# Refilling buffers two tiles further ahead in a LayerNorm and GELU kernel that streams 128 MB

## The chip, the cores and the metric

The kernel runs on one core of one Trainium2 chip. The metric is the device time of one execution in microseconds (us), taken as the median of several executions. The span that the profile gives, from the first to the last instruction, is 1.7 to 1.8 us shorter than the time. "The trace" below is the record of one execution: instructions, DMA packets, and the semaphore updates that tell when a transfer has landed.

## The reference, cut to what matters

```python
mean = np.mean(x, axis=-1, keepdims=True)             # x: 8 x 1024 x 2048 float32
var = np.var(x, axis=-1, keepdims=True)
normalized = (x - mean) / np.sqrt(var + eps)
out = gamma * normalized + beta
return 0.5 * out * (1 + np.tanh(np.sqrt(2 / np.pi) * (out + 0.044715 * out ** 3)))
```

The input is 64 MB and the output is 64 MB. As 128-row tiles of 128 x 2048 float32 these are 64 tiles of 1 MB each way.

## The kernel before

Twenty tile buffers (`NB = 20`) rotate. A tile is loaded into its buffer, its mean and variance are taken there (VectorE, and ScalarE for one tile in four of most groups), VectorE writes (x - mean) * gamma to PSUM, TensorE adds the beta term, ScalarE applies the GELU back into the same buffer, and SyncE stores the buffer. SyncE issues all loads and stores, in program order:

```python
NB = 20
LAG = 4
...
def load(i):
    xt = xin.tile([P, d], F32, name="xt")
    nc.sync.dma_start(out=xt, in_=xf[i * P:(i + 1) * P])          # L53
    xts[i] = xt
...
for i in range(NB):
    load(i)
...
def gelu(j):
    g, k = of_tile[j]
    nc.scalar.activation(out=xts[j], in_=ps[j % 2], func=ACTF.Gelu_apprx_tanh,
                         scale=rstds[g][0][:, k:k + 1])            # L151
    nc.sync.dma_start(out=of[j * P:(j + 1) * P], in_=xts[j])       # L153
    nxt = j + NB - LAG
    if NB <= nxt < ntiles:
        load(nxt)
```

Behind the store of tile j stands the load of tile j+16. It goes into the buffer of tile j-4, so it may start only when the store of tile j-4 has landed. SyncE waits there, and whatever stands behind that load in its list waits with it.

## Time and profile before

| | before |
|---|---|
| time, median of the first 3 runs | 325.29 us (324.59 to 325.31) |
| span of the profiled run | 323.2 us |
| busy: DVE, PE, ACT, POOL | 85%, 80%, 63%, 41% |
| packet time of the DMA queue, share of 16 engines | 98.8% |
| traffic | 134.2 MB, 415 GB/s over the span |
| landing of the last store | 322.24 us |

The first reading is that DMA is full and no compute engine is. The lines of the profile themselves stand in the prediction.

### The profile page before, as it was taken

To read this page: it belongs to the slowest core of one execution; us is meant where nothing else is said; L and a number is where in the kernel's file an instruction comes from. 1 tells how busy PE (TensorE), PEld (TensorE's weight loads), DVE (VectorE), ACT (ScalarE), POOL (GpSimd) and SP (SyncE) were. 2 spreads that over 40 slices of the span, in tenths; PEclk is the share of its full clock that TensorE was granted. 3 is DMA by queue.
4 is the path that set the end of the run, shared out by engine and by line. 5 is a ranking of instruction groups with operands and counts; after the bars stand their busy time and mean duration, and the time that the engine had idled before them with its cause. 6 is when DMAs were issued, how large, how long until landed. Compare 5 with 4: busy or idle time off the path is not lost.

```text
span 323.2 us, 2327 instructions
## 1 busy us (share of the span) xinstructions
PE 258.3 (80%) x528; PEld 100.9 (31%) x528; DVE 276.3 (85%) x315; ACT 203.7 (63%) x188; POOL 132.2 (41%) x319
## 2 busy tenths in 40 slices
PE   5978548888888888988888877858988588888890
PEld 2423223333333333333333323323333133333330
DVE  2989968989999999999999969966998789997520
ACT  1237557678778686868777776744687476544552
POOL 0732231827180807171635342050361505488800
PEclk9999958999999999999999999978999799999998
DMA  7999999999999999999999999999999999999994
GB/s 295 425 424 422 422 419 425 428 410 429 427 428 426 427 427 425 428 425 426 427 427 428 425 429 430 421 427 431 424 429 428 426 425 429 426 426 426 425 394 197
DMA packets 18450, 134.39 MB, mean 416 GB/s; under 512 B 2050, under 2 KB 2050, under 8 KB 2050
## 3 DMA queue, kind: packets, MB, share of 16 engines
q1 hardware_dynamic: 18432, 134.23, 98.8%
q8 instruction: 4, 0.07, 0.1%
q14 instruction: 10, 0.08, 0.1%
q10 hardware_dynamic: 4, 0.02, 0.0%
HBM read 67.13 MB, written 67.11 MB: 415 GB/s over the span
## 4 chain that ended last, share of the span: by engine, by line
DVE 46%; DMA 25%; PE 9%; issue 8%; POOL 5%; ACT 4%; DVEq 0%; SPq 0%; POOLq 0%; ACTq 0%
DVE ps L142 26%; DMA xt<-in_x_dram 24%; DVE st L100 18%; PE ps L146 5%; PE ps L75 4%; ACT xt L151 3%; DVE mv L102 2%; POOL t L127 2%; DMA g_t<-in_gamma_dram 1%; POOL std L130 1%; POOL y L129 1%; ACT b_t L76 1%; POOL t L126 1%; POOL t L128 1%; ACT w L136 0%
## 5 line engine op out<-in xcount | busy, mean ns | idle before, releaser
L146 PE MATMUL ps<-b_t,w 128*128 128x512 f32 x512 | 244.3, 623 | 53.0 <-DVE ps L142 43.0
L151 ACT ACTIVATE xt<-ps,y 128x2048 f32<-128x2048 f32 x64 | 125.9, 1967 | 89.5 <-PE ps L146 87.1
L142 DVE SCALAR_TENSOR_TENSOR ps<-xt,mv,g_t 128x2048 f32<-128x2048 f32 x64 | 149.4, 2334 | 18.1 <-ACT xt L151 16.7
L146 PEld LDWEIGHTS ps<-b_t,w 128*128 128x128 f32 x512 | 95.7, 196 | 202.3 <-issue 120.9
L100 DVE BATCH_NORM_STATS2 st<-xt 128x6 f32<-128x512 f32 x200 | 125.9, 672 | 13.2 <-DMA xt<-in_x_dram 13.0
L112 POOL TENSOR_SCALAR mv<-sq 128x1 f32<-128x1 f32 x14 | 8.7, 619 | 117.2 <-ACT junk L111 117.2
L126 POOL TENSOR_TENSOR t<-y 128x4 f32<-128x4 f32 (+2 forms) x60 | 48.3, 805 | 4.8
L111 ACT ACTIVATE junk<-xt,mv 128x2048 bf16<-128x2048 f32 x14 | 27.9, 1991 | 0.0
L106 ACT ACTIVATE junk<-xt 128x2048 bf16<-128x2048 f32 x14 | 26.6, 1900 | 0.0
L136 ACT ACTIVATE w<-ident,std 128x128 f32<-128x128 f32 x64 | 20.5, 389 | 9.4 <-POOL std L130 9.4
L127 POOL TENSOR_TENSOR t<-t,ve 128x4 f32<-128x4 f32 (+2 forms) x60 | 22.3, 372 | 4.7
L128 POOL TENSOR_SCALAR t<-t 128x4 f32<-128x4 f32 (+2 forms) x60 | 21.8, 364 | 5.2
L122 POOL TENSOR_SCALAR ve<-mv 128x4 f32<-128x4 f32 (+2 forms) x20 | 4.6, 231 | 34.4 <-DVE mv L102 34.0
L129 POOL TENSOR_TENSOR y<-y,t 128x4 f32<-128x4 f32 (+2 forms) x60 | 14.0, 234 | 5.0
L102 DVE BATCH_NORM_AGGREGATE mv<-st 128x2 f32<-128x24 f32 x50 | 13.2, 264 | 2.8
L75 PE MATMUL ps<-g_t,ones 1*128 1x512 f32 x8 | 7.2, 1072 | 3.7 <-DMA g_t<-in_gamma_dram 3.7
L75 PE MATMUL ps<-b_t,ones 1*128 1x512 f32 x8 | 7.0, 1056 | 0.0
L76 ACT ACTIVATE g_t<-ps 128x2048 f32<-128x2048 f32 x1 | 1.9, 1877 | 7.8 <-PE ps L75 7.8
L130 POOL TENSOR_TENSOR std<-ve,y 128x4 f32<-128x4 f32 (+2 forms) x20 | 6.0, 302 | 1.6
L123 POOL TENSOR_SCALAR y<-ve 128x4 int32<-128x4 int32 (+2 forms) x20 | 6.0, 299 | 1.7
L76 ACT ACTIVATE b_t<-ps 128x2048 f32<-128x2048 f32 x1 | 1.9, 1877 | 4.9 <-PE ps L75 4.9
L75 PEld LDWEIGHTS ps<-g_t,ones 1*128 1x128 f32 x8 | 2.5, 325 | 6.8 <-issue 6.8
(11 smaller groups left out, 10.3 us busy)
## 6 DMA issues: line engine op xcount, KB each, us to landing
xt<-in_x_dram SPq DMA_DIRECT2D x64, 1024.0 KB, 19.7
out_dram<-xt SPq DMA_DIRECT2D x64, 1024.0 KB, 19.6
g_t<-in_gamma_dram ACTq DMA_DIRECT2D x1, 8.0 KB
b_t<-in_beta_dram ACTq DMA_DIRECT2D x1, 8.0 KB
```

What stands on the lines that cost most here:

```text
L75: nc.tensor.matmul(pt[:, s], lhsT=ones[0:1, :], rhs=row[0:1, s], start=True, stop=True)
L100: nc.vector.bn_stats(out=sts[i][:, c, :], in_=xts[i][:, c * BANK:(c + 1) * BANK])
L102: nc.vector.bn_aggr(out=slot(i), in_=sts.pop(i))
L106: nc.scalar.activation(out=junk, in_=xts[i], func=ACTF.Identity, scale=-1.0 / d, accum_out=slot(i)[:, 0:1])
L111: nc.scalar.activation(out=junk, in_=xts[i], func=ACTF.Square, bias=slot(i)[:, 0:1], accum_out=sq)
L126: po.tensor_tensor(out=t, in0=y, in1=y, op=MUL)
L127: po.tensor_tensor(out=t, in0=t, in1=ve, op=MUL)
L128: po.tensor_scalar(out=t, in0=t, scalar1=-0.5, scalar2=1.5, op0=MUL, op1=ADD)
L136: nc.scalar.activation(out=w, in_=ident, func=ACTF.Identity, scale=rstds[g][1][:, k:k + 1])
L142: nc.vector.scalar_tensor_tensor(out=pt, in0=xts[j], scalar=mvs[g][:, k, 0:1], in1=g_t, op0=ADD if j in on_scalar else SUB, op1=MUL)
L146: nc.tensor.matmul(pt[:, s], lhsT=wts[j], rhs=b_t[:, s], start=False, stop=True, skip_group_check=True)
L151: nc.scalar.activation(out=xts[j], in_=ps[j % 2], func=ACTF.Gelu_apprx_tanh, scale=rstds[g][0][:, k:k + 1])
```

## The change

The intent is to ask for a tile earlier: behind the store of tile j SyncE loads tile j+18, into the buffer that tile j-2 leaves. Loads then run two tiles further ahead of the stores, and two fewer stores stand ahead of each of these later loads, called refills below.

```diff
     NB = 20
-    LAG = 4
+    LAG = 2
     GAP, SLACK = 3, 7
```

## The prediction

> **What bounds the kernel now.** I read four views in this order: the page, the table of stages by window, the waits of SyncE's queue, and the chain that ended last. The page first: which resource is full.
>
> ```profile
> PE 258.3 (80%) x528; PEld 100.9 (31%) x528; DVE 276.3 (85%) x315; ACT 203.7 (63%) x188; POOL 132.2 (41%) x319
> ...
> DMA  7999999999999999999999999999999999999994
> ...
> q1 hardware_dynamic: 18432, 134.23, 98.8%
> ...
> xt<-in_x_dram SPq DMA_DIRECT2D x64, 1024.0 KB, 19.7
> out_dram<-xt SPq DMA_DIRECT2D x64, 1024.0 KB, 19.6
> ```
>
> The reader is to see that the 16 DMA engines are full from the second slice to the last but one, that one queue carries everything (64 loads and 64 stores of 1 MB), and that VectorE, the busiest compute engine, is 15% idle. Each transfer takes some 19.7 us from issue to landing. The trace records when each one landed: the first load at 6.08 us, the last store at 322.24, so 127 steps in 316.16 us, 2.49 us each. One engine's share of a transfer is 8 packets of 8 KB, and the median packet takes 0.309 us: 8 x 0.309 = 2.47 us. So from first landing to last there is almost no slack. 19.7 / 2.47 = 8.0 transfers are in flight.
>
> Then where the DMA engines are not full (columns: window; its length; busy time and count for PE, PEld, DVE, ACT, POOL; the clock; the DMA share; GB/s):
>
> ```profile
> 100.00:260.00 160.00, 132.46 (x280) 51.81 (x279) 147.90 (x168) 112.06 (x103) 63.35 (x144) 0.97 1.01 427
> 260.00:312.00 52.00, 45.18 (x100) 17.69 (x99) 42.56 (x41) 30.32 (x27) 29.59 (x61) 1.00 1.01 426
> 312.00:318.00 6.00, 3.01 (x8) 0.98 (x6) 0.00 (x0) 2.69 (x2) 0.00 (x0) 1.00 0.67 279
> 318.00:323.20 5.20, 0.00 (x0) 0.00 (x0) 0.00 (x0) 0.00 (x0) 0.00 (x0) 0.71 0.45 186
> ```
>
> Only the last 11 us show idle DMA time: 0.33 x 6.0 + 0.55 x 5.2 = 4.8 us on the mean of the 16 engines. This is all that an earlier load could win back, if anything can.
>
> Then why SyncE issues when it does (waiter <- what ended it: us in total, times, longest):
>
> ```profile
> SPq L53 <- DMA xt<-in_x_dram: 95.4, 48, 2.1
> SPq L153 <- DMA out_dram<-xt: 85.9, 42, 2.7
> SPq L153 <- ACT xt L151: 47.5, 17, 5.5
> ...
> SPq L53 <- DMA out_dram<-xt: 3.6, 2, 2.5
> ```
>
> A load (L53) waits for an earlier load 48 times, and for a store only twice, although the code makes it wait for the store that leaves its buffer. The trace tells which: the load of tile 45, issued at 172.94, follows the landing of the load of tile 41 at 172.87, eight transfers earlier in SyncE's order. Every transfer n waits for transfer n-8 here, as the eight completion semaphores are used in turn. The buffer wait is hidden behind that: load j+16 needs store j-4, nine places earlier, which has landed by then.
>
> Last, the chain, in order of time (start, length, what):
>
> ```profile
> 232.27 19.80 DMA xt<-in_x_dram
> 252.09 0.69 DVE st L100
> 252.79 2.27 DVE ps L142
> ...
> 311.34 3.69 PE ps L146 x8
> 315.05 1.97 ACT xt L151
> ```
>
> From 172.94 to 252.09 the chain is load after load. At 252.09 the load of tile 57 lands, VectorE has waited 2.73 us for it, and from there compute runs to the last Gelu at 317.02, 64.9 us later. The last store is then issued and lands 5.2 us later. The chain says that the end hangs on when tile 57 arrives. I don't follow it there, for the reason under "the end" below.
>
> **What the Trainium skill says.** "DMA: Bandwidth & Descriptors", section "Why a DMA increments its semaphore by 16 and not by 1", says that a transfer's engines finish independently and that only the full count means landed. The trace agrees: the sixteen completions of the store of tile 61 came between 312.55 and 317.33 us, 4.8 us apart. The same page, section "Anatomy of one DMA", says "DMA engines do not wait on semaphores" and that the wait lies in the issuing sequencer; the trace agrees, with 181 us of SyncE waits on earlier transfers while the DMA share stays at 1.01. Its section "Bandwidth" has 425 GB/s for a 16 MB load on a lone core; this trace holds 426 to 427 with loads and stores mixed, so there is no higher rate to hope for. "Perfetto Trace Analysis", section "What 'DMA-bound' means", lists being bound on specific DMA engines as one case. My argument turns on that.
>
> **The change, part by part.** Instructions of the four compute engines stand in the same order in both kernels; only SyncE's list moves: three stores instead of five stand before the first refill, and eighteen instead of sixteen after the last load. No byte and no instruction is added.
>
> *The wait.* With LAG 2 SyncE's order is store j-2, load j+16, store j-1, load j+17, store j, load j+18, and the last waits for the first, five places earlier. This wait now binds in place of the eight-deep one. When it ends, four transfers are left in the queue, then a load and a store go out together: 4 to 6 in flight in place of 8. Landing should take about 4 to 5 transfers, 10 to 12.5 us, in place of 19.7. That alone saves and costs nothing as long as no DMA engine runs dry.
>
> *Does one run dry?* Four transfers are 4 x 2.47 = 9.9 us of work for the engine that is last. The others are ahead by up to 4.8 us (from the spread above), so they have at least 5.1 us left. A new transfer's overhead, read from the last store, which met mostly empty engines, is: issue 317.04 to the middle completion 320.81 = 3.77 us, less 2.47 of data, 1.3 us. 5.1 is well above 1.3. The thinnest place is the first refill: store 0 lands at 56.06 with only stores 1 and 2 behind it, the middle completions of which came at 57.62 and 60.05. Load 20 goes out at 56.13 as before, needed by about 59; store 3 follows 0.4 us later, and load 21 when store 1 lands, at 58.50. Some 1.5 to 2 us to spare there. Cost: 0.
>
> *The loads.* Each refill has two fewer stores ahead of it, so it lands 2 x 2.47 = 4.9 us earlier: tile 57 at 247.1 instead of 252.07. VectorE's wait at tile 45 (2.56 us) should vanish; those at tiles 49 and later shift with the loads. Compute then ends at 317.0 - 4.9 = 312.1.
>
> *The stores.* They go out later, and buffers spend their time as finished output waiting for SyncE instead of in the DMA queue. No compute waits for a store: Gelu writes in place, and only a load needs the buffer back.
>
> *The end.* Here I chose between two readings of those last 11 us. The mean engine is idle for 4.8 us, but the landing of a store is that of its slowest engine: stores 61, 62 and 63 landed at 317.33, 319.83 and 322.24, steps of 2.50 and 2.41 us, which is full pace. The middle completions of the same stores came at 313.70, 316.54 and 320.81, with gaps. So one engine, 4.8 us behind (it took instruction fetches between its packets: one of 8 KB at 283.16 us, where the spread grows from 3.57 to 4.21), works without a pause to the end, and its 128 x 8 packets are the same after the change. Compute ending at 312.1 fills the pauses of the other engines, which then finish near 311.26 + 3 x 2.45 = 318.6 (from the middle completion of store 60), and the slow one still lands the last store at about 322.2. Gain: 0, up to 3.6 us only if the lag itself shrank.
>
> Sum: 0 (bulk) + 0 (queue depth) + 0 to -3.6 (end, most likely near 0) = 325.3, and I take 0.3 off for the chance of the latter: 325.0 us.
>
> **The rivals.** *The end follows compute.* If the last store's pace were set by its issue, the 4.9 us of earlier compute would come through up to the 3.6 us above: about 321.7 us. For it: the chain, and the idle shares of 0.33 and 0.55. Against: the full-pace steps of the last landings. I give it one in eight. *The shallow queue runs dry.* If SyncE's wait cost a pause for each refill of, say, 0.3 us, 43 of them make 13 us: 338 us. For it: SyncE now stands behind a store's completion, and nothing else can be issued meanwhile. Against: the 5.1 us left against 1.3. I give it 3%. *Stores held back stall compute.* Compute would wait if a buffer came free too late, but the refill comes earlier in the order, not later, and tile 45's wait goes. That would give the same 325.
>
> **Range and chances.** The three runs before spread over 0.7 us. The lag of one engine can differ by one instruction fetch, about 0.7 us either way. With one in eight for the first rival, 323.0 to 326.3 should hold it 8 times in 10. Even full success of that rival is -1.1%, so faster by over 2% (below 318.8) has 1%; slower has 3%; within 2% has 96%.
>
> **What would show it.** Right: landing times of 10 to 13 us; loads that now wait mostly for a store; the DMA share at 1.01 up to about 316 us or beyond, and then a sharper fall; the last Gelu some 5 us earlier (312); the last stores' landings still 2.4 to 2.5 us apart; the span near 323. Wrong: DMA shares below 1.0 in the middle (the queue ran dry), or the last landing near 318.6 (the lag was a product of the deep queue, not of the engine).

## The result, and the profile after

| | before | after |
|---|---|---|
| time, median of 6 runs each | 325.26 us (324.59 to 325.43) | 324.14 us (324.06 to 324.63) |
| span of the profiled run | 323.2 us | 322.4 us |
| last GELU ends | 317.02 us | 311.83 us |
| last store lands | 322.24 us | 321.43 us |

The ratio is 0.9975, with a 95% interval of 0.9962 to 0.9988. Ratios are the mean time of one kernel's runs over that of the other's runs of the same rounds, so they are not quite the ratio of the medians in the table. Executions over 1.5% slower than the fastest of the same kernel are left out of the means. By the 2% rule the two kernels are the same; a small difference of about 0.8 us is outside the noise.

The page after, the parts that answer to those shown of before (DMA share by slice, the queue, the transfers with their time from issue to landing):

```profile
DMA  7999999999999999999999999999999999999994
...
q1 hardware_dynamic: 18432, 134.23, 99.0%
...
xt<-in_x_dram SPq DMA_DIRECT2D x64, 1024.0 KB, 12.3
out_dram<-xt SPq DMA_DIRECT2D x64, 1024.0 KB, 14.4
```

The DMA engines are as full as before, and each transfer spends 12 to 14 us on its way in place of 19.7. So the queue is shorter, five or six transfers in place of eight, and nothing was lost by it.

The stages by window (columns as in the prediction):

```profile
100.00:260.00 160.00, 135.81 (x289) 53.10 (x290) 151.79 (x172) 116.81 (x109) 67.26 (x144) 0.98 1.01 427
260.00:312.00 52.00, 44.11 (x96) 17.07 (x96) 38.74 (x38) 28.66 (x23) 29.29 (x61) 1.00 1.01 427
312.00:318.00 6.00, 0.00 (x0) 0.00 (x0) 0.00 (x0) 0.00 (x0) 0.00 (x0) 0.56 0.92 391
318.00:322.40 4.40, 0.00 (x0) 0.00 (x0) 0.00 (x0) 0.00 (x0) 0.00 (x0) 0.50 0.10 43
```

The third window in two parts:

```profile
312.00:316.00 4.00, 0.00 (x0) 0.00 (x0) 0.00 (x0) 0.00 (x0) 0.00 (x0) 0.59 1.01 426
316.00:318.00 2.00, 0.00 (x0) 0.00 (x0) 0.00 (x0) 0.00 (x0) 0.00 (x0) 0.50 0.76 320
```

The middle holds the same 427 GB/s. In the window from 312 to 318 all compute is over, where before PE and ACT still worked, and the DMA share has risen from 0.67 to 0.92; the engines are full up to 316 us. In return it falls to 0.10 in the last window: most DMA engines are done, and the core waits for the last one. The earlier compute bought a fuller tail for the engines that were not the last.

SyncE's waits after (waiter <- what ended it: us in total, times, longest):

```profile
SPq L53 <- DMA out_dram<-xt: 178.3, 44, 14.5
SPq L53 <- DMA xt<-in_x_dram: 25.0, 12, 2.2
...
SPq L153 <- ACT xt L151: 13.0, 10, 3.9
```

Now each of the 44 refills waits for a store, which only 2 did before. SyncE spends 178 us in that wait and it costs nothing, since the DMA engines work meanwhile.

Parts of the chain that ended last, after (start, length, what):

```profile
234.58 12.30 DMA xt<-in_x_dram
246.90 0.69 DVE st L100
...
309.86 1.97 ACT xt L151
```

The load of tile 57 lands at 246.9 us and not at 252.1, and the whole compute tail moves with it, by 5.2 us. The time moved by about 1. This is what the next part tests.

### The profile page after: what moved, and what is told of

The parts are those of the page before. It is cut to its first block, busy times and chain, and to the rows that moved or that the text cites. A ratio compares the mean times of both kernels' runs of the same rounds, so it can differ in the third digit from the quotient of the medians.

```text
span 322.4 us, 2297 instructions
## 1 busy us (share of the span) xinstructions
PE 257.6 (80%) x528; PEld 100.5 (31%) x528; DVE 276.0 (86%) x315; ACT 203.7 (63%) x188; POOL 135.8 (42%) x319
## 4 chain that ended last, share of the span: by engine, by line
DVE 59%; PE 11%; DMA 9%; issue 9%; POOL 5%; ACT 4%; DVEq 0%; POOLq 0%; SPq 0%; ACTq 0%
DVE ps L142 33%; DVE st L100 23%; PE ps L146 6%; DMA out_dram<-xt 4%; PE ps L75 4%; DMA xt<-in_x_dram 4%; ACT xt L151 4%; DVE mv L102 2%; POOL t L127 2%; DMA g_t<-in_gamma_dram 1%; POOL std L130 1%; ACT b_t L76 1%; POOL y L129 1%; POOL t L126 1%; POOL t L128 1%
## 5 line engine op out<-in xcount | busy, mean ns | idle before, releaser
L126 POOL TENSOR_TENSOR t<-y 128x4 f32<-128x4 f32 (+2 forms) x60 | 54.3, 904 | 4.8
L129 POOL TENSOR_TENSOR y<-y,t 128x4 f32<-128x4 f32 (+2 forms) x60 | 16.1, 268 | 5.0
L127 POOL TENSOR_TENSOR t<-t,ve 128x4 f32<-128x4 f32 (+2 forms) x60 | 16.0, 267 | 4.7
L130 POOL TENSOR_TENSOR std<-ve,y 128x4 f32<-128x4 f32 (+2 forms) x20 | 8.1, 407 | 1.6
## 6 DMA issues: line engine op xcount, KB each, us to landing
xt<-in_x_dram SPq DMA_DIRECT2D x64, 1024.0 KB, 12.3
out_dram<-xt SPq DMA_DIRECT2D x64, 1024.0 KB, 14.4
```

What stands on the lines that cost most here:

```text
L126: po.tensor_tensor(out=t, in0=y, in1=y, op=MUL)
L127: po.tensor_tensor(out=t, in0=t, in1=ve, op=MUL)
```

## The experiments

Eleven kernels ran, in three groups; kernels of one group shared a chip and the runs of the kernel before. Landing times are read from the sixteen completions that the trace records for each transfer, one from each DMA engine; "lands" means the last of them, and "the middle" is their median. The trace doesn't number the engines. That the same one comes last from transfer to transfer is read from its even steps and the slowly growing spread of the completions.

**Theory.** The end is set by the DMA engine that finishes last, which works through its 128 shares of 8 packets without a pause. LAG moves waits and compute about, and the time does not follow as long as that engine is fed and compute does not end too late. **Rivals.** Compute's end sets the time. A shorter queue lowers the rate. The small gain comes from something else than the loads.

### Compute's end on the other side: LAG 6 and LAG 5

```diff
-    LAG = 2
+    LAG = 6
```

> LAG 6: the store that a load waits for is thirteen places back and never binds; the queue is eight deep as before; loads land two stores, 4.9 us, later than before. If compute's end counts on this side, it moves from 317.0 to 321.9 us, the last store lands 3.8 to 5.2 us later, at 325.7 to 327.1, and the time is about 328.5 to 330 (+1.2%). If the DMA engines alone set the end: 325.3 again.

Measured: 328.93 us (328.25 to 329.84, 4 runs), ratio to before 1.0125 (1.0107 to 1.0143). Its trace, the end of the chain and the last two windows:

```profile
320.13 1.97 ACT xt L151
```

```profile
312.00:318.00 6.00, 5.25 (x12) 2.30 (x13) 2.36 (x1) 4.14 (x3) 0.42 (x3) 1.00 0.60 249
318.00:326.90 8.90, 2.09 (x5) 0.57 (x3) 0.00 (x0) 1.97 (x1) 0.00 (x0) 0.75 0.57 236
```

The last GELU ends at 322.1 us, and the last store lands at 325.97, 3.85 us after it was issued. All sixteen completions of that store come within 0.15 us, so no DMA engine has a backlog any more: compute ends so late that the late engine has caught up, as far as these times tell. Here compute sets the end.

LAG 5 (the same edit with 5) is the step between.

> LAG 5: loads land one store, 2.5 us, later than before. On the side of LAG 6 the last landing followed the last Gelu by 3.9 us; if that rule holds from LAG 4's 317.0 + 2.5 = 319.5, the last landing is at 323.3 and the time about 326.3 us, half way between before (325.0) and LAG 6 (328.9) or a little less. If LAG 4 were already clearly bound by compute, it would be 327.0.

Measured: 326.17 us (325.28 to 327.18, 6 runs), ratio 1.0040 (1.0025 to 1.0056). The last store is issued at 319.50 and lands at 323.34 us, again 3.84 us later and with all sixteen together. So the rule on this side is: the end is the last GELU plus 3.85 us. With before's last GELU at 317.0 it gives 320.9, and before's last store lands at 322.24, set by the late engine. The changeover lies where the last GELU ends at 322.2 - 3.85 = 318.4 us, between LAG 4 and LAG 5. Before had 1.4 us to spare, and by this rule moving compute earlier could give nothing.

### No compute at all

The whole body between the first twenty loads and the stores is taken out, and each loaded tile is stored as it is. The result is wrong.

```diff
 def gelu(j):
-    nc.scalar.activation(...)
     nc.sync.dma_start(out=of[j * P:(j + 1) * P], in_=xts[j])
...
+for j in range(ntiles):
+    gelu(j)
```

> Wrong on purpose: LAG 2 with all compute taken out, each loaded tile stored as it is. 128 transfers by 2.47 us from a first landing at 6.1 us is 320 us. DMA theory: the time falls by 1 to 3 us only, to 321 to 323 (the rest of the lag, from fetches of the compute engines' instructions, is gone). If compute or the order of waits had a share in the end beyond that: clearly below 320.

Measured: 321.74 us (321.22 to 322.23, 4 runs), ratio 0.9897 (0.9882 to 0.9912). Its windows (columns: window, length, POOL, clock, DMA share, GB/s):

```profile
100.00:260.00 160.00, 0.00 (x0) 1.00 1.01 427
260.00:312.00 52.00, 0.00 (x0) 1.00 1.01 428
312.00:318.00 6.00, 0.00 (x0) 1.00 0.86 362
318.00:320.50 2.50, 0.00 (x0) 1.00 0.03 13
```

Taking away all of the compute saves 3.3 us of 325, and the rate in the middle is the same 427 GB/s. That is the strongest evidence that the bytes, not the compute, bound both kernels. SyncE's waits are not tested by it: the 44 waits of refills for stores are still there, 180.1 us in all. Its trace also has one packet of instructions of 8 KB or more where LAG 2 has thirteen before its end (these fetches come up again below); how much of the 3.3 us they make up is not shown. The engine that finishes last is still there: the middle of the last store's completions is at 317.65 us and the last at 319.68.

### A shorter queue still: LAG 1 and LAG 0

```diff
-    LAG = 2
+    LAG = 1
```

> LAG 1: a load waits for the store three places earlier, so two transfers are left in the queue when the wait ends, 4.9 us of work for the engine that is last against 1.3 us of overhead. DMA theory: the last engine never runs dry, 324.1 to 324.7, while engines ahead by over 3.6 us pause, so that the spread between engines stays under about 4 us. Queue-depth rival (throughput needs many transfers in flight): some per cent slower.

Measured: 359.60 us (355.41 to 359.90, 3 runs; the fourth, 364.33, was slow), ratio 1.1008 (1.0943 to 1.1072). My expectation was wrong, and the rival of the shorter queue was right at this depth. The stretch from 100 to 250 us, first with LAG 2, then with LAG 1:

```profile
100.00:250.00 150.00, 126.92 (x273) 49.46 (x273) 143.25 (x163) 110.62 (x102) 63.59 (x137) 0.99 1.01 427
```

```profile
100.00:250.00 150.00, 116.78 (x238) 46.23 (x237) 123.38 (x139) 94.96 (x88) 41.40 (x119) 0.92 0.99 361
```

The DMA share is 0.99, as if the engines were full, and the rate is 361 GB/s in place of 427. So the loss is not idle time between packets; the packets themselves take longer. Between 90 and 250 us the mean packet of 8 KB took 0.360 us, against 0.3095 with LAG 2, and the slowest took 2.4 us.

Which packets? SyncE's issues in the timeline of the trace with LAG 1 (start, length, what):

```profile
93.17 0.34 SPq L53 DMA_DIRECT2D xt<-in_x_dram  x1
93.56 0.46 SPq L153 DMA_DIRECT2D out_dram<-xt  x1
98.08 0.34 SPq L53 DMA_DIRECT2D xt<-in_x_dram  x1
98.47 0.70 SPq L153 DMA_DIRECT2D out_dram<-xt  x1
105.00 0.34 SPq L53 DMA_DIRECT2D xt<-in_x_dram  x1
```

The distances alternate, 4.9 us and 6.9 us. The load issued at 93.17 landed 4.43 us after the store ahead of it; the load issued at 98.08 landed 2.40 us after the one ahead of it, which is the normal pace; the load of 105.00 took 4.66 again. What I find to differ between them is how long before its turn a load was issued. I take as its lead the time from its issue until the first DMA engine has finished the transfer ahead. In this trace, over the loads that SyncE refills:

```
lead of the load        loads   step from the transfer ahead (middle completion)
1.0 to 2.1 us           21      3.1 to 4.8 us
2.8 to 5.9 us           23      2.1 to 2.8 us
LAG 2: 3.9 to 8.7 us    44      2.2 to 2.5 us
```

There is nothing between, and no overlap. In this trace a load that an engine reaches 2.1 us or less after its issue runs slowly; from 2.8 us on it runs at full pace. Stores don't show this: seven stores, in the traces of LAG 3, LAG 5, LAG 6 and the three with LAG 4 (two of before, and "LAG 4 then 2" below), had leads of 0.5 to 2.0 us and stepped 2.4 to 2.6 us. With LAG 2 the smallest lead is 3.9 us, at the first refill, and from the second on at least 6.1. Within one run and with the same code the two kinds alternate, which speaks against the clock or the chip as the reason. That the lead is what matters is read from this one trace; I did not set leads by themselves. What an engine does in those slow packets, the trace does not say.

LAG 0 (the same edit with 0) takes away any lead.

> LAG 0: each load waits for the store just issued, in the same buffer, so the queue empties once for each of 44 pairs. A pair then takes 2 x 2.47 us and the turn-round of a landing, 1.3 to 2 us, in place of 4.93: 44 x 1.3 to 2 is 57 to 88 us more, 380 to 412 us. If it were far less, the overhead per landing that I reckon with would be too large.

Measured: 508.98 us, one look, state unknown. The expectation of 380 to 412 was too low, for the same reason:

```profile
100.00:400.00 300.00, 155.91 (x269) 61.44 (x267) 141.96 (x157) 110.83 (x102) 29.45 (x144) 0.77 0.71 227
```

A load here takes 6.6 us from issue to landing on an empty queue (median), where the last store of LAG 6 took 3.85 on an empty queue. Less the 2.47 us of data, a load has 4.1 us of overhead here and a store 1.4. I had taken the store's figure for both. Nor is a load's figure one number: the first load of each of the thirteen traces, also on an empty queue, took 4.6 to 4.8 us to its middle completion, where the loads of LAG 0 took 6.0. Why, these runs don't show. A load and a store after it now take about 6.6 + 2.5 = 9.1 us in place of 4.93; 44 such pairs make 183 us more, and 325 + 183 = 508 us is close to the 508.98 measured.

### Where the 0.8 us come from

The second question is small, but the first result is outside the noise. In the trace of before, SyncE's list had 236 instructions, after it 205. The difference lies in its separate wait instructions: before stores they fell from 62 to 21, before loads they rose from 34 to 44. The traces show packets of 8 KB of the kind "instruction" between the data. One of them comes when SyncE has reached about its instruction 81 and the next at about 209 (208 to 210), in the kernels with a longer and a shorter list alike, so I take these for fetches of SyncE's own instructions. So with 236 instructions a fetch falls at 283.2 us, and with 205 only after the end, at 323.9. Four kernels of one group test this.

The changed kernel once more:

> The changed kernel once more, as the yardstick of this call: 324.1 us (324.0 to 324.7), 0.8 to 1.1 us under before, under every theory. The question for the other three runs is where this small difference comes from.

Measured: 324.39 us (324.26 to 324.50, 5 runs), before 325.02 in the same group, ratio 0.9983 (0.9971 to 0.9996). The difference is there again, 0.6 us.

Padding SyncE's list back to its old length, behind the first twenty loads:

```diff
     for i in range(NB):
         load(i)
+    for _ in range(31):
+        nc.sync.drain()
```

> LAG 2 with 31 idle instructions (drains) added to SyncE's list behind the first twenty loads, where it waits anyway: as many as the change took away (236 against 205 in the trace). Theory A, the 0.8 us come from an 8 KB instruction fetch of SyncE that falls before the end only when its list is longer than 208: the fetch is back, near 280 us, on the DMA engine that ends last, and the time rises by 0.6 to 0.8 us to about 324.9. Theory B, they come from compute ending 5 us earlier or from the shorter queue: unchanged, 324.1.

Measured: 324.53 us (324.24 to 324.64, 5 runs), ratio 0.9986 (0.9974 to 0.9999). The fetch is back, at 282.65 us, and the spread of the completions grows by 0.6 us there. But the time rose by 0.14 us and not by 0.6 to 0.8, and the five runs of the two kernels overlap. By its own number this expectation was missed; the time is nearer to what the rival, theory B, foresaw.

LAG 3:

```diff
-    LAG = 2
+    LAG = 3
```

> LAG 3: SyncE's list is one instruction longer than with LAG 2, so no fetch of it before the end; loads come 2.5 us earlier than before instead of 4.9. Theory A: the same as LAG 2, 324.1. Theory B (compute's end, or the depth of the queue): half of the gain, about 324.7.

Measured: 324.22 us (324.04 to 324.39, 5 runs), ratio 0.9979 (0.9965 to 0.9992). LAG 3 is as fast as LAG 2, so the gain is not in proportion to how much earlier the loads come. Its list has 206 instructions.

Gamma and beta shared out over all DMA engines:

```diff
-    g_t = singles.tile([P, d], F32)
-    nc.scalar.dma_start(out=g_t[0:1, :], in_=gamma.unsqueeze(0))
+    g_p = singles.tile([P, 16, 132], F32)
...
+    for row, vec in ((g_p, gamma), (b_p, beta)):
+        nc.scalar.dma_start(out=row[0:1, :, 0:P], in_=vec.unsqueeze(0).rearrange("p (a b) -> p a b", a=16))
```

> LAG 2, and gamma and beta loaded as sixteen rows of 512 bytes into a padded row, so that all 16 DMA engines share them instead of one carrying both 8 KB packets. Theory A (the end is the queue of one DMA engine, the one that was 0.9 us late since its two packets of gamma and beta): that engine ends about 1.0 us earlier, 323.1. Rival (the lag is not of that engine, or the end isn't set by one engine): unchanged, 324.1.

Measured: 324.48 us (324.20 to 324.63, 5 runs), ratio 0.9985 (0.9972 to 0.9997). (The first matmuls read the padded rows.) Nothing was gained. In the trace gamma and beta now come as 32 packets of 512 bytes in place of two of 8 KB, and the completions of the last store still lie 4.5 us apart, in the repeated LAG 2 4.3. So these two packets are not what makes one engine last at the end.

Two more kernels in the last group. The kernel before, with its own trace:

> The kernel before once more, with its own trace, for the 0.6 to 0.9 us that the earlier runs of LAG 2 and 3 are under it: 325.0 us (324.5 to 325.4). If the difference lies in the last 16 transfers, these take 40.3 us or more here as in the first trace of before (40.46), against 39.3 to 39.8 in the traces of LAG 2 and 3. If instead this trace is like theirs, the difference is no fixed part of the kernel's end.

Measured: 325.20 us (324.70 to 325.23, 5 runs), ratio 1.0003 (0.9991 to 1.0015).

LAG 4 for three quarters and LAG 2 at the end:

```diff
-        nxt = j + NB - LAG
-        if NB <= nxt < ntiles:
-            load(nxt)
+        lag = LAG if j < 40 else 2
+        while len(xts) <= j + NB - lag and len(xts) < ntiles:
+            load(len(xts))
```

> LAG 4 up to store 39, then two loads more in one go, and LAG 2 to the end: SyncE's list stays nearly as long as before's (five fewer), the loads of the last five groups come early as in LAG 2. If the difference comes from compute's end or the state of the queue in the last quarter: 324.3 us, like LAG 2. If from the length of SyncE's list or from the first three quarters: 325.0, like before.

Measured: 325.32 us (324.55 to 325.44, 5 runs), ratio 1.0005 (0.9992 to 1.0018). So the gain doesn't come from the last quarter's loads alone; the length of the list and the first three quarters remain. It issues its last store at 314.56 us, 2.5 us before the first trace of before does (317.04), and that store lands at 322.67. The second trace of before issues it at 315.79 and lands it at 322.54. Three ends of compute, 2.5 us apart, and landings within 0.43 us: at LAG 4 the end is not compute's.

Side by side, with the last 16 transfers measured from landing 112 to landing 128:

```
kernel         SyncE's list   fetch of SyncE near the end   last 16 transfers   time (us)
before              236       283.2 us                      40.46 us            325.26
before again        236       283.5                         40.43               325.20
LAG 4 then 2        231       289.6                         40.35               325.32
LAG 2 padded        236       282.7                         40.31               324.53
LAG 2               205       after the end                 39.79               324.14
LAG 2 again         205       after the end                 39.72               324.39
LAG 2, gamma        205       after the end                 39.71               324.48
LAG 3               206       after the end                 39.34               324.22
```

Every trace with a late fetch has the longer tail, by 0.5 us or more, and every trace without it the shorter. For the tail the theory of the fetch holds in all eight. For the whole time it holds in seven: the padded kernel has the long tail and yet nearly the short time. In its trace the 110th transfer had landed at 276.22 us, where the other seven have 276.6 to 277.3 (276.8 to 277.3 with LAG 4, 276.6 to 277.2 with LAG 2 and 3, so the first three quarters don't tell these apart). Its last engine had lost less until then (the profiled run was also the fastest of its five). Why, I cannot say. So the fetch is seen in the tail; but the one run that put it back alone did not bring the time back, so that it is the cause of the 0.8 us is not shown, and the cause stays open.

None of these versions beats LAG 2 or LAG 3, which are equal within their spread.

## Why the prediction was right

The time of 324.14 us lies in the range of 323.0 to 326.3, 0.9 us under the number given. That the time would hardly move was reasoned, and the reasons held. That it fell by 0.8 us was not forecast; the range allowed for it, with "about 0.7 us either way" for one instruction fetch. Step by step:

- **The wait.** Right in kind: all 44 refills wait for a store. The transfers' way was put at 10 to 12.5 us; loads took 12.3, stores 14.4. The count was short by one or two: the load goes out behind four transfers and is itself the fifth, the store behind it the sixth.
- **Does an engine run dry?** The answer, no, was right: 427 GB/s before and after. (That there is no higher rate to hope for doesn't follow from one measured rate; in the windows of 50 us or more looked at here none was above 428.) The reasoning had a flaw. The overhead of 1.3 us was read from a store on an empty queue and used for loads, which need a lead of between 2.1 and 2.8 us in the trace of LAG 1. LAG 2 leaves 3.9 us at the thinnest place and 6.1 or more elsewhere, so the flaw did no harm here; that there was still room for a load was luck as far as the reasoning went. With LAG 1 the same reasoning missed a loss of 10%.
- **The loads and compute's end.** Tile 57 was put at 247.1 us and landed at 246.9; the last GELU was put at 312.1 and ended at 311.8.
- **The end.** The middle completion of the last store was put at 318.6 us and came at 318.62. The slow engine was put at about 322.2 and came at 321.43. The mechanism fits, and the experiments bear it out from both sides: compute counts only beyond 318.4 us (LAG 5, LAG 6), and its absence gives only 3.3 us. The term that was off is the slow engine's lag. I took it as the same after the change; its last 16 transfers took 0.67 us less. In the same stretch a fetch of SyncE's instructions is gone, but that this is the cause is not shown.
- **The rivals.** "The end follows compute" would have given 321.7 us and did not come. "The shallow queue runs dry" was given 3% at LAG 2; it did not come there, but it is real one step further, though its cost there is in the packets of late loads and not in idle time. "Stores held back stall compute" did not come: compute ended 5.2 us earlier, and the one wait of ScalarE for a store, 2.4 us, is in both traces.
- **The sign to look for.** "The DMA share at 1.01 up to about 316 us or beyond, and then a sharper fall": it came, with 1.01 from 312 to 316, 0.76 from 316 to 318 and 0.10 after that, and the last landings are still 2.4 us apart (316.55, 318.99, 321.43 us).

## What to carry to other kernels

When DMA is full, look at which DMA engine completes the last transfers before crediting an earlier compute: the mean idle share of the tail can belong to engines that do not decide. A prefetch distance can have a nearly flat middle and two edges, here LAG 2 to 4; one edge is where compute's end shows, the other where a load is issued too shortly before its turn, and the second was far steeper (10% at LAG 1, 1.2% at LAG 6). Read the rate beside the DMA share, since engines can look full and be slow.

## What the Trainium skill lacked or had wrong

- "DMA: Bandwidth & Descriptors" has a first-byte figure of some 600 ns for transfers from SyncE, in "Latency and other measured facts", and no figure for how early a load must be queued. Here (LAG 1) a 1 MB load that was reached 2.1 us or less after its issue took 3.1 to 4.8 us in place of 2.45, and at 2.8 us or more about the normal step.
- The same page, section "Anatomy of one DMA", fits one fixed cost of about 2.0 us for transfers from GpSimd, and says that the delay of the completion can be surprisingly long when the target is HBM; for transfers from SyncE it has no figures by direction. Here the loads were the dearer: on an empty queue a 1 MB store took 3.85 us from issue to landing (LAG 6) and a load 6.6 us (LAG 0, median; the first load of a trace 4.8 to 5.7), of which 2.47 us is data in each case.
- "Perfetto Trace Analysis", section "Identifying the Most-Contended Engine", says to use the memory's utilization instead of occupancy for DMA. This agrees and gives it a number: a DMA share of 0.99 at 361 GB/s (LAG 1) against 1.01 at 427 GB/s.
- "Runtime: NRT & Kernel Launch", section "Instruction fetch mechanics", says that a sequencer fetches ahead over its own DMA queue, in blocks of 16 KiB, at a cost that is mostly hidden. No page has what that takes from the DMA engines of a DMA-bound kernel. Here fetches came as packets of 8 or 16 KB between the data, 0.31 to 1.1 us each, those taken for SyncE's of 8 KB; the traces whose last 16 transfers hold one of SyncE's took 40.3 to 40.5 us there against 39.3 to 39.8.
